# A hybrid four-mixer backbone on one core: own buffers for the gated branch, a fixed buffer layout, and other TensorE prices for the kernel's list scheduler

## The chip, the core and the metric

The kernel runs on one core of one Trainium2 chip. The metric is device time in microseconds (us) of one execution. Five engines work side by side, each in its own instruction order: TensorE (PE, matmuls; its weight loads appear as PEld), VectorE (DVE), ScalarE (ACT), GpSimd (POOL, here only an issuer of DMAs) and SyncE (SP, an issuer of DMAs).

## What is computed

Two layers work on 512 latent and 256 context tokens of width 1024. Each layer normalises and modulates its input to `h`, projects it, runs four token mixers side by side, and merges them through sigmoid gates:

```python
h = rmsnorm(x, norm_gain[l]) * (1.0 + scale) + shift
za, zb, zh, zf, zg = jnp.split(h @ w_in[l], SPLIT_IDX, axis=-1)
ya, yca = mixer_diff_attn(za, ...)     # differential attention, axial rotary
yb, ycb = mixer_neigh_attn(zb, ...)    # neighbourhood attention with a position bias
yh, ych = mixer_hgrn2(zh, ...)         # gated linear recurrence, both directions
yf = fourier_mix(zf)
x = x + gate * merge_branches(h, (ya, yb, yh, yf), zg, w_up[l], w_merge[l], w_out[l])

def merge_branches(h, ys, g, w_up_l, w_merge_l, w_out_l):
    for i in range(N_BRANCH):
        branch = (ys[i] * jax.nn.silu(gs[i])) @ w_up_l[i]
        term = jax.nn.sigmoid(h @ w_merge_l[i]) * branch
        acc = term if acc is None else acc + term
    return acc @ w_out_l
```

The context tokens go through the same weights; layer 1 needs them only as keys, values and state. Everything is float32.

## The kernel before

The large products are made three times over in the reduced float32 form (high x high, high x low, low x high): `split` (ACT for the high part, DVE for the low part) makes the two parts of each operand, and `mm3` issues the three products for each 128-row block. `h` is kept transposed in `h_hi` and `h_lo`. Weights arrive by SP into two buffers `wraw`, and are split into four buffers each of `wh` and `wl` ahead of their use. A product with `h` as the moving operand has 384 or 512 columns (`gemm_a`), one with a slice of `h` or of the merged result as the stationary operand has 256 (`gemm_b`, and the output projection).

The order of a layer as the program writes it: the projections of the recurrence, Fourier and differential branches; then four `merge` calls, one for each branch (Fourier, recurrence, differential, neighbourhood), with the projection of the neighbourhood branch (NA) ahead of the third; then the output projection, in whose last part the norm of the next layer begins. The four branches are generators (`ft_mix`, `hg_mix`, `da_mix`, `na_mix`); after each large product `unit_done` lets them take steps, and `need` completes a branch before its merge. NA starts once its keys are projected, so its steps lie beside the third merge, that of the differential branch.

`merge` (L1472) first makes the gated branch: gate product, tanh into `mth` (2 buffers), two DVE products, and a split into `ygs`, four tiles from the common buffers "u". Then for each of eight blocks it makes a merge-gate product, its tanh, an up projection of `ygs`, and adds to `acc`. In some blocks a set of eight 32-row matmuls makes modulation rows of the next layer or the output gate (`mod_rows`, by tiles `psg<-u,cst`).

None of this is the order that the chip runs. Each call is recorded as an `Op` (consecutive PE calls on one tile are one; `mm3` is cut into atoms of 4 x 3 matmuls), and `Program.order` is a list scheduler: again and again it takes the instruction that can start first, in the program's order among equals (weight transfers and splits count as 400 instructions earlier), by the prices in `Program.price` (L229) and by latencies. It looks at most 300 instructions past the oldest that is not done. An instruction that opens a new tile of a group ("tag") is taken only if a buffer is free and if the number of live tiles, counted in the program's order from the oldest open instruction on, stays within the buffers (`ok` in `order`). The most used group is "u", 31 buffers (`SLOTS`, L40) of 3072 bytes in each partition. The chosen order is emitted for each engine, which then runs strictly in it.

`emit` gives tiles their place in SBUF in the order of their first use, each padded to 32 bytes, behind 16384 bytes of descriptor space for POOL's DMAs. In the program so built, `wraw`, `wh` and `wl` start at multiples of 128 bytes, `h_hi` and `h_lo` 64 bytes past one, and the "u" buffers 96 bytes past one. PSUM is split into `psg` (3 buffers, large products), `psw` (2) and `pst` (1), for the branches.

Of the kernel before, what the change touches and what calls it, by code (L numbers as in the profile page):

```python
# [11 lines left out]
F32 = mybir.dt.float32  # L12
F32R = mybir.dt.float32r
# [8 lines left out]
P = 128  # L22
# [3 lines left out]
NT = NX + NC  # L26
# [10 lines left out]
MAIN_IN = (W_HF0, W_HQ, W_HI, W_FT, W_HF1, W_DAK, W_DAQ, W_DAV)  # L37
MERGE_ORDER = (3, 2, 0, 1)
NA_AT = 2
SLOTS = 31  # L40
RAW_BUFS = 2
W_BUFS = 4
PACE = 1.8
LEVELS = (64, 32, 16, 8, 4, 2, 1)
NA_KS = (0, 8, 24, 32)
NA_VAR = (0, 1, 1, 2)


class Tile:
# [120 lines left out]
class Program:  # L170
# [58 lines left out]
    def price(self, engine, method, args, kw):  # L229
        o = args[0]  # L230
        if method == "dma_start":
            return {"gpsimd": 1.0, "sync": 0.45, "scalar": 0.1}[engine]
        n = math.prod(o.shape[1:])
        if engine == "tensor":
            if method == "transpose":
                return 4 * args[1].shape[0] / 2400
            m = o.shape[0]
            slow = 4 if n >= m else 8 * m / n
            if args[2].dt != F32R and min(m, args[2].shape[0]) <= 64:
                slow = 2 * max(1, m / n)  # L240
            if args[2].dt == F32R:
                slow = 1 if n >= 2 * m else slow
            return (slow * n + 6) / 2400
        ins = [v for v in args[1:] if isinstance(v, View)]
        ps = any(v.tile.space == "ps" for v in ins + [o])
        n = max([n] + [math.prod(v.shape[1:]) for v in ins])
        if engine == "scalar":
            more = sum(isinstance(kw.get(k), View) for k in ("accum_out", "bias", "scale"))
            return (0.055 if ps else 0.095) + 0.09 * more + n / 1200
        two = len([v for v in ins if math.prod(v.shape[1:]) > 1]) > 1 or method == "tensor_reduce"  # L250
        if method == "reciprocal":
            return 0.07 + n / 160
        return 0.07 + n / (960 if two or ps else 1920)
# [82 lines left out]

    def emit(self, nc, pools):
        order = self.order()
        for op in order:
            for t in op.tiles:  # L340
                if t.real is None:
                    t.real = pools[t.space].tile(t.shape, t.dt, tag=t.tag, bufs=t.bufs, name=t.name)
            f = lambda v: v.real() if isinstance(v, View) else v
            for engine, method, args, kw in op.calls:
                getattr(getattr(nc, engine), method)(*map(f, args), **{k: f(v) for k, v in kw.items()})  # L345
        self.time = max(op.end for op in order)
# [3 lines left out]
def tile_hybrid_mixers(ctx, tc, io, out, dump=None):  # L350
    pools = {
        "sb": ctx.enter_context(tc.tile_pool(name="sb", bufs=1)),
        "ps": ctx.enter_context(tc.tile_pool(name="ps", bufs=1, space=PSUM)),
        "dram": ctx.enter_context(tc.tile_pool(name="dram", bufs=1, space=DRAM)),
    }
    ctx.enter_context(tc.manual_schedule())
    nc = Program()
# [9 lines left out]
    def nm(s):  # L367
        count[0] += 1
        return f"{s}_{count[0]}"

    def slot(shape=(P, NT), dt=F32):
        return mp.tile(list(shape), dt, tag="u", bufs=SLOTS, name=nm("u"))

# [36 lines left out]
    cols = cpool.tile([P, CO_N], F32, name="cols")  # L410
# [7 lines left out]
    masks = cpool.tile([P, len(LEVELS), P], I8, name="masks")  # L418
# [625 lines left out]
    def na_mix(l, z, res):  # L1044
# [2 lines left out]
        gn = sp.tile([P, 128], F32, tag="ngain", bufs=1, name=nm("ngain"))  # L1047
        nc.gpsimd.dma_start(gn, io["na_gain"][l:l + 1].partition_broadcast(P).rearrange("p a d -> p (a d)"))
        ts(gn[:, 0:64], gn[:, 0:64], 0.125)
        yT = [slot() for _ in range(2)]  # L1050
        res[1] = yT
        ntok = (6 if full else 4, 6)
        for i in (1, 0):
            yield from wait_for((l, "na", i))
            n = (3, ntok[i] - 3)
# [8 lines left out]
        for b in range(2):  # L1064
# [28 lines left out]
            k1, q1, q2 = (slot(dt=F32R) for _ in range(3))  # L1093
# [47 lines left out]
            def turn(cb, es):  # L1141
                w = 512 if cb < 4 else 256
                ps = psw()
                out = []
                for h in range(2):
                    for k in range(w // P):
                        transpose(ps[:, 512 * h + P * k:512 * h + P * (k + 1)], es[h][:, P * k:P * (k + 1)])
                for h in range(2):
                    eT = slot([P, 512])
                    act(eT[:, 0:w], ps[:, 512 * h:512 * h + w])  # L1150
                    out.append(eT)
                return out
# [319 lines left out]
    def merge(l, br, res, acc, first, last, fin, between):  # L1472
        rng = a_ranges(l == 0)
        wh, wl = chunk()
        yT = None
        ygs = [[slot(dt=F32R) for _ in range(2)] for _ in range(2)]
        for b in range(2):
            for n0, n1 in rng:
                ps = gemm_a(wh, wl, slice(P * b, P * (b + 1)), n0, n1)
                th = sp.tile([P, 512], F32, tag="mth", bufs=2, name=nm("mth"))[:, 0:n1 - n0]  # L1480
                act(th, ps, AF.Tanh, scale=0.5)
                stt(th, th, 1.0, ps, ALU.add, ALU.mult)
                stt(th, th, 0.5, res[br][b][:, n0:n1], ALU.mult, ALU.mult)
                split(ygs[b][0][:, n0:n1], ygs[b][1][:, n0:n1], th)
                unit_done(0.0103 * (n1 - n0))
        up = None
        for db in range(8):
            if db % 4 == 0:
                weights.release()
                if up is not None:  # L1490
                    weights.drop(1)
                up = [x.rearrange("p (b k c) -> p b k c", b=4, k=2) for x in weights.take()]
            wh, wl = chunk(1)
            if first:
                acc[db] = slot()
            if last:
                fin[db] = [slot(dt=F32R) for _ in range(2)]
            for n0, n1 in rng:
                ps = gemm_a(wh, wl, slice(0, P), n0, n1)
                th = sp.tile([P, 512], F32, tag="mth", bufs=2, name=nm("mth"))[:, 0:n1 - n0]  # L1500
                act(th, ps, AF.Tanh, scale=0.5)
                pu = psg()[:, 0:n1 - n0]
                mm3(pu, [(up[0][:, db % 4, k, :], up[1][:, db % 4, k, :], ygs[k][0][:, n0:n1], ygs[k][1][:, n0:n1]) for k in range(2)])
                a = acc[db][:, n0:n1]
                if first:
                    stt(a, th, 1.0, pu, ALU.add, ALU.mult)
                else:
                    stt(th, th, 1.0, pu, ALU.add, ALU.mult)
                    if last:
                        tt(th, th, a, ALU.add)  # L1510
                        split(fin[db][0][:, n0:n1], fin[db][1][:, n0:n1], th)
                    else:
                        tt(a, a, th, ALU.add)
                unit_done(0.0129 * (n1 - n0))
            between(db)
        weights.release()
        weights.drop(1)
# [6 lines left out]
    for l in range(DEPTH):  # L1524
# [44 lines left out]
        for j in range(4):  # L1569
            gt = gates[j]  # L1570
            cs = slice(256 * j, 256 * (j + 1))
            for u in range(2):
                n = min(3, nt - 3 * u)
                xn[j, u] = slot([P, 3, 256])
                nc.gpsimd.dma_start(xn[j, u][:, 0:n, :], xsrc[384 * u:384 * u + P * n, cs].rearrange("(t p) d -> p t d", p=P))
            wh, wl = chunk()
            for t in range(nt):
# [4 lines left out]
                u = sp.tile([P, 2, 256], F32, tag="q2", bufs=2, name=nm("gu"))[:, 0, :]  # L1582
# [127 lines left out]
```

## Time and profile before

| | |
|---|---|
| runs | 1517.60, 1518.24, 1518.64 us; median 1518.24 us |
| profiled execution | 1520.19 us, of which the span of its instructions 1518.4 us |
| PE busy | 1457.1 us, 96% of the span |
| DVE, ACT busy | 953.6 us (63%), 628.5 us (41%) |
| TensorE clock granted, mean | 0.988 of full |

The profile is one execution. Times in it count from the span's start. A tile `u<-mth` is an instruction that writes a tile of the group `u` and reads one of the group `mth`; since a helper records every operation, all instructions have the line L345, and tiles tell them apart. Matmul durations overlap, so how fast PE goes is read from the distance of starts or from the number in a stretch.

### The profile page before, as it was taken

The numbers are of one execution on the slowest core, as the hardware profiler recorded it, in microseconds if no ns is written. First come the engines' busy times: TensorE is split into PE (matmuls) and PEld (weight loads), VectorE is DVE, ScalarE is ACT, GpSimd is POOL, SyncE is SP. The second block draws the span as 40 slices with busy tenths as digits, with TensorE's granted clock in tenths as the row PEclk, the third lists the DMA queues.
The fourth block names the chain that finished last, engine by engine and source line by source line (L and its number), as shares of the span: only waits on it lengthen the run. The fifth ranks groups of instructions, "written<-read, shape, count | busy, mean of one in ns | idle before, by whom it ended". The sixth has DMA issues, their size and how long they took to land.

```text
span 1518.4 us, 25432 instructions
## 1 busy us (share of the span) xinstructions
PE 1457.1 (96%) x10068; PEld 1331.9 (88%) x10068; DVE 953.6 (63%) x2058; ACT 628.5 (41%) x1384; POOL 106.7 (7%) x207
## 2 busy tenths in 40 slices
PE   3999999999999997999999999999999999999998
PEld 2899989889999997889999999898887889888788
DVE  7794988577553355643444467979967855673544
ACT  5344454466522243431323244436445634552330
POOL 1000002210000010100001110000131000110000
PEclk9999999999999998999999999999999999999999
DMA  9211012332322142362222331211253222545332
GB/s 350 109 43 43 32 57 70 85 85 91 115 77 70 53 107 93 75 218 74 80 73 92 113 103 57 70 33 56 70 134 98 88 83 84 136 132 176 101 111 74
DMA packets 50599, 144.76 MB, mean 95 GB/s; under 512 B 7280, under 2 KB 12400, under 8 KB 50480
## 3 DMA queue, kind: packets, MB, share of 16 engines
q1 hardware_dynamic: 38336, 112.21, 22.7%
q0 software_dynamic: 12144, 30.93, 8.0%
q8 instruction: 79, 1.29, 0.3%
q14 instruction: 40, 0.33, 0.1%
HBM read 123.98 MB, written 4.19 MB: 84 GB/s over the span
## 4 chain that ended last, share of the span: by engine, by line
PE 85%; DVE 6%; ACT 5%; issue 2%; DMA 1%; SPq 0%; ACTq 0%; DVEq 0%; POOLq 0%
PE psg L345 69%; PE psw L345 11%; PE pst L345 4%; DVE u L345 3%; ACT u L345 3%; DVE sm L345 2%; ACT wh L345 1%; DMA u<-in_xin_dram 1%; ACT mth L345 0%; DVE wl L345 0%; DMA u<-in_rpb_dram 0%; DVE nss L345 0%; DVE psw L345 0%; SPq L345 0%; ACT h_hi L345 0%
## 5 line engine op out<-in xcount | busy, mean ns | idle before, releaser
L345 PE MATMUL psg<-h_hi,wh 128*128 128x384 f32 (+2 forms) x1216 | 439.6, 362 | 4.0 <-ACT mth L345 2.8
L345 PE MATMUL psg<-h_lo,wh 128*128 128x384 f32 (+2 forms) x1216 | 430.3, 354 | 0.2 <-DVE h_lo L345 0.2
L345 PE MATMUL psg<-h_hi,wl 128*128 128x384 f32 (+2 forms) x1216 | 430.4, 354 | 0.0
L345 DVE TENSOR_TENSOR wl<-wraw,wh 128x512 fp32r<-128x512 f32 x312 | 201.7, 686 | 175.8 <-ACT wh L345 174.9
L345 ACT ACTIVATE wh<-wraw 128x512 fp32r<-128x512 f32 x312 | 180.2, 624 | 244.7 <-PE psg L345 218.7
L345 PEld LDWEIGHTS psg<-h_hi,wh 128*128 128x128 f32 x1216 | 230.1, 189 | 24.9 <-ACT mth L345 5.7
L345 PEld LDWEIGHTS psg<-h_hi,wl 128*128 128x128 f32 x1216 | 229.8, 189 | 15.8
L345 PEld LDWEIGHTS psg<-h_lo,wh 128*128 128x128 f32 x1216 | 230.4, 189 | 14.8 <-DVE h_lo L345 0.5
L345 PE MATMUL psg<-wh,h_hi 128*128 128x256 f32 x544 | 156.3, 287 | 0.0
L345 PE MATMUL psw<-u,u 64*128 64x128 f32 (+6 forms) x1144 | 141.2, 299 | 12.3 <-ACT u L345 7.5
L345 PE MATMUL psg<-wl,h_hi 128*128 128x256 f32 x544 | 151.0, 278 | 0.0
L345 PE MATMUL psg<-wh,h_lo 128*128 128x256 f32 x544 | 150.9, 277 | 0.0
L345 ACT ACTIVATE u<-psw 128x768 f32<-128x768 f32 (+12 forms) x248 | 114.4, 485 | 81.3 <-PE psw L345 72.7
L345 PEld LDWEIGHTS psw<-u,u 64*128 64x128 f32 (+2 forms) x1144 | 113.1, 192 | 28.3 <-ACT u L345 13.2
L345 ACT ACTIVATE u<-psw,sm 128x768 f32<-128x768 f32 (+2 forms) x120 | 90.6, 758 | 88.9 <-DVE sm L345 75.7
L345 PE MATMUL psg<-wh,u 128*128 128x256 f32 x640 | 114.2, 280 | 0.9 <-ACT mth L345 0.9
L345 ACT ACTIVATE mth<-psg 128x384 f32<-128x384 f32 (+1 forms) x120 | 62.1, 519 | 127.8 <-PE psg L345 120.4
L345 DVE SCALAR_TENSOR_TENSOR mth<-mth,psg 128x384 f32<-128x384 f32 (+1 forms) x96 | 57.1, 595 | 91.0 <-ACT mth L345 73.9
L345 PE MATMUL psg<-u,wh 128*128 128x384 f32 (+1 forms) x384 | 107.6, 361 | 0.2 <-DVE u L345 0.2
L345 DVE TENSOR_REDUCE sm<-psw 128x1 f32<-128x768 f32 (+3 forms) x100 | 89.5, 901 | 26.1 <-PE psw L345 25.6
L345 PEld LDWEIGHTS psg<-wh,h_hi 128*128 128x128 f32 x544 | 102.2, 188 | 4.0
L345 POOL DMA_DIRECT2D u<-u x132 | 65.1, 505 | 568.8 <-ACT u L345 343.0
(128 smaller groups left out, 2002.9 us busy)
## 6 DMA issues: line engine op xcount, KB each, us to landing
wraw<-in_w_merge_dram SPq DMA_DIRECT2D x64, 512.0 KB, 3.6
wraw<-in_w_in_dram SPq DMA_DIRECT2D x60, 512.0 KB, 3.8
u<-in_w_mod_dram SPq DMA_DIRECT2D x32, 384.0 KB, 7.0
wraw<-in_w_up_dram SPq DMA_DIRECT2D x16, 512.0 KB, 3.5
wraw<-in_w_out_dram SPq DMA_DIRECT2D x16, 512.0 KB, 4.2
u<-u POOLq DMA_DIRECT2D x72, 96.0 KB, 2.4
u<-in_w_gate_dram SPq DMA_DIRECT2D x16, 384.0 KB, 6.3
u<-u POOLq DMA_DIRECT2D x24, 192.0 KB, 2.6
```

The source lines that it names most:

```text
L345: getattr(getattr(nc, engine), method)(*map(f, args), **{k: f(v) for k, v in kw.items()})
```

## The change

- The gated branch's four tiles get buffers of their own (group `yg`, 4 buffers of 3072 bytes).
- NA's output takes the buffer `dd` (6144 bytes), which the recurrence used alone before; NA's transposed attention weights take the two buffers `q2`, used so far by the rotary step and the output projection.
- "u" has 29 buffers instead of 31. The descriptor space of POOL's DMAs is 8192 bytes instead of 16384.
- Twelve groups get their place in SBUF first, in the order of the list `LAYOUT`.
- The scheduler's PE prices: a transpose has half its price; a reduced-form matmul costs its columns + 32 cycles of 2.4 GHz instead of columns + 6 (or four times the columns, where these were under twice the rows); one with at most 32 output rows costs its columns + 16 instead of twice the columns; others are as before up to a few cycles, and half where the output is one or two columns wide. The other engines' prices and the latencies stay.

```diff
-SLOTS = 31
+SLOTS = 29
+LAYOUT = ("cols", "masks", "ls2", "wraw", "wh", "wl", "ldl4", "nlam1", "hhi", "hlo", "u", "yg")
@@ price
             if method == "transpose":
-                return 4 * args[1].shape[0] / 2400
+                return 2 * args[1].shape[0] / 2400
             m = o.shape[0]
-            slow = 4 if n >= m else 8 * m / n
-            if args[2].dt != F32R and min(m, args[2].shape[0]) <= 64:
-                slow = 2 * max(1, m / n)
             if args[2].dt == F32R:
-                slow = 1 if n >= 2 * m else slow
-            return (slow * n + 6) / 2400
+                return (n + 32) / 2400
+            if m <= 32:
+                return (n + 16) / 2400
+            return (2 if min(m, args[2].shape[0]) <= 64 else 4) * max(n, m) / 2400
@@ emit
         order = self.order()
+        first = {}
+        for op in order:
+            for t in op.tiles:
+                first.setdefault(t.tag, t)
+        for tag in LAYOUT:
+            t = first[tag]
+            t.real = pools[t.space].tile(t.shape, t.dt, tag=t.tag, bufs=t.bufs, name=t.name)
@@ na_mix
-        yT = [slot() for _ in range(2)]
+        pair = mp.tile([P, 2, NT], F32, tag="dd", bufs=1, name=nm("yna"))
+        yT = [pair[:, b] for b in range(2)]
@@ na_mix, turn
-                    eT = slot([P, 512])
+                    eT = sp.tile([P, 512], F32, tag="q2", bufs=2, name=nm("eT"))
@@ merge
-        ygs = [[slot(dt=F32R) for _ in range(2)] for _ in range(2)]
+        ygs = [[mp.tile([P, NT], F32R, tag="yg", bufs=4, name=nm("yg")) for _ in range(2)] for _ in range(2)]
@@ kernel
-    nc = bacc.Bacc("TRN2", target_bir_lowering=False, num_devices=1)
+    nc = bacc.Bacc("TRN2", target_bir_lowering=False, num_devices=1, dynamic_dma_scratch_size=8192)
```

## Rows read from the trace of the kernel before

**Rows 1.** The page, busy us of each engine, share of the span, instructions.
```profile
PE 1457.1 (96%) x10068; PEld 1331.9 (88%) x10068; DVE 953.6 (63%) x2058; ACT 628.5 (41%) x1384; POOL 106.7 (7%) x207
```

**Rows 2.** Waits of PE, whole span: us in total, times, longest.
```profile
PE psg L345 <- DVE sm L345: 19.4, 1, 19.4
PE psw L345 <- ACT u L345: 18.1, 23, 2.9
...
PE psg L345 <- ACT mth L345: 6.6, 14, 0.5
```

**Rows 3.** Table of stretches: busy us (instructions), granted clock, DMA share, GB/s.
```profile
core 0: us, PE busy (x) PEld busy (x) DVE busy (x) ACT busy (x) POOL busy (x), PEclk, DMA share, GB/s
580.00:590.00 10.00, 10.00 (x66) 9.84 (x64) 5.03 (x10) 3.57 (x8) 0.00 (x0) 1.00 0.41 133
...
280.00:310.00 30.00, 25.94 (x157) 22.71 (x156) 19.57 (x42) 16.51 (x37) 5.58 (x12) 0.83 0.27 66
...
590.00:620.00 30.00, 21.18 (x140) 18.59 (x140) 16.55 (x35) 13.68 (x36) 2.31 (x5) 0.72 0.12 28
0.00:50.00 50.00, 25.34 (x210) 17.02 (x211) 36.71 (x95) 26.03 (x40) 5.66 (x14) 0.94 0.91 327
```

**Rows 4.** Timeline of DVE and ACT: start, length, instruction, idle before and its releaser.
```profile
406.53 0.56 DVE L345 SCALAR_TENSOR_TENSOR mth<-mth,u 128x384 f32<-128x384 f32 x1
...
407.12 0.53 ACT L345 ACTIVATE u<-mth 128x384 fp32r<-128x384 f32 x1 [0.80 <-DVE mth L345]
...
576.77 0.54 DVE L345 SCALAR_TENSOR_TENSOR mth<-mth,u 128x384 f32<-128x384 f32 x1
...
592.43 0.69 ACT L345 ACTIVATE u<-psw,sm 128x512 f32<-128x512 f32 x1 [4.29 <-DVE sm L345]
...
606.20 0.94 ACT L345 ACTIVATE u<-mth 128x384 fp32r<-128x384 f32 x2
```

**Rows 5.** Timeline of PE from 588 to 604 us.
```profile
588.94 1.11 PE L345 MATMUL psw<-u,u 128*128 128x256 f32 x8
...
593.93 1.97 PE L345 MATMUL psw<-kc,u 128*128 128x128 f32 x8 [2.86 <-ACT u L345]
597.08 2.08 PE L345 MATMUL psw<-u,u 128*128 128x256 f32 x8 [1.18 <-ACT u L345]
...
603.37 1.76 PE L345 MATMUL psw<-kc,u 128*128 128x128 f32 x8 [2.66 <-ACT u L345]
```

**Rows 6.** Chain that ended last, two pieces of large products: start, us, matmuls.
```profile
579.90 6.25 PE psg L345 x36
...
610.38 3.94 PE psg L345 x12
```

**Rows 7.** Timelines of PE and ACT: transposes; modulation rows, and ACT beside them.
```profile
557.79 1.47 PE L345 MATMUL psw<-kc,u 128*128 128x128 f32 x12
...
464.68 1.07 PE L345 MATMUL psg<-u,cst 128*32 128x256 f32 x16
466.24 0.61 PE L345 MATMUL psg<-kc,mrow 128*128 128x2 f32 x4 [0.49 <-ACT mth L345]
...
464.66 1.15 ACT L345 ACTIVATE wh<-wraw 128x512 fp32r<-128x512 f32 x2 [0.98 <-ACT wh L345]
```

**Rows 8.** Table of stretches: NA's projection, and the output projection of layer 0.
```profile
520.00:540.00 20.00, 20.00 (x179) 20.00 (x178) 10.24 (x22) 7.20 (x14) 0.00 (x0) 1.00 0.16 53
840.00:860.00 20.00, 20.00 (x173) 20.00 (x173) 9.88 (x31) 5.88 (x20) 3.25 (x6) 1.00 0.28 83
```

**Rows 9.** PE's groups by shape, output projections: busy us, mean ns of one.
```profile
L345 PE MATMUL psg<-wh,u 128*128 128x256 f32 x640 | 114.2, 280 | 0.9 <-ACT mth L345 0.9
L345 PE MATMUL psg<-wl,u 128*128 128x256 f32 x320 | 89.4, 279 | 0.0
```

**Rows 10.** The page: one kind of DMA issue with median us to landing; POOL's queue, packets, MB.
```profile
u<-in_w_mod_dram SPq DMA_DIRECT2D x32, 384.0 KB, 7.0
...
q0 software_dynamic: 12144, 30.93, 8.0%
```

## The prediction

> **What bounds the kernel now.** I read the page's busy shares first: TensorE (PE) is busy in 96% of the span, VectorE in 63% [rows 1]. So time goes away only where PE waits or where its work becomes faster; 1518.4 - 1457.1 = 61.3 us of the span is PE idle. Next, PE's list of waits [rows 2]: 19.4 us is one wait in the opening, before the first data is there; the rest lies in many waits on ScalarE (ACT) evictions, in stages where a branch's steps run between the large matmuls. Then the table of stretches [rows 3], which shows where they gather. From 580 to 590 us PE is full at the upper clock level. From 590 to 620 us it is busy 21.18 of 30 us, so 8.82 us idle, and the granted clock is 0.72: a mix of the two levels, 2.4 and 1.2 GHz. The only comparable stretch behind the opening is 280 to 310 us (4.06 us idle, 0.83).
>
> Last, the timelines of VectorE and ACT say why 590 to 620 us is so poor [rows 4]. In `merge`, after the gate's second product (`mth<-mth,u`) comes the split into the gated branch's high and low part (`u<-mth`). At 406 us the split starts 0.03 us after that product. The one made at 576.77 us ends at 577.31 and is split at 606.20, 28.9 us later, while ACT has idle time in between (4.29 us before one exponential); an earlier gate's split is in the same pair of splits at 606.20. Product and ACT were free, so what was missing is the target: those tiles come from the 31 buffers "u", and in that stage the neighbourhood attention (NA) of layer 0 holds them; counted by program order, all 31 are live there and at most 28 outside NA. The planner may not issue an instruction whose new tile would exceed the count. The gate temporaries (2 buffers `mth`) and PSUM tiles (3 `psg`) then fill up, no gate matmul can run, and PE is left with NA's own chain of scores, maximum, exponential, transpose, values: its transposes come at 593.93 and 603.37, one round in 9.4 us, with 2.86 and 2.66 us idle before them [rows 5].
>
> **Part by part.**
> *Own buffers for the gated branch (`yg`), NA's output in `dd`, its transposed weights in `q2`.* The split can then follow its product, the gates and up projections of that merge fill the chain's gaps, and the clock has no idle stretch to fall in. Worth at most: the 8.82 us idle, plus what ran slowly: the 8 score matmuls 2.08 instead of 1.11 us (+0.97), 8 transposes 1.97 and 1.76 instead of 8/12 of 1.47, that is 0.98 (+0.99 and +0.78) [rows 5, 7], 12 gate matmuls 3.94 instead of a third of 6.25, that is 2.08 (+1.86) [rows 6]. Sum 4.6, so 13.4 us. I take 12, as a covered chain still leaves short waits; the other end is 0. What moves forward is work that PE has to do anyway, and behind this stage PE is full with merges, so nothing else is late next. The transposed weights' two buffers add a wait: the eviction of a round needs the values of the round before to be done. PE runs values before the next transposes already (values sit between 588.94 and 593.93 [rows 5]); if it did bind, it costs the eviction's queue on ACT at most one group of score matmuls' length, 1.1 us, in the two or three rounds that are bound by the chain: 0 to 3 us, taken as 0. NA's output in `dd` waits for the recurrence of the same layer, which is complete before the second merge, and NA begins in the third: nothing.
>
> *Addresses (`LAYOUT`, smaller descriptor scratch).* Buffers are laid down in the order of first use, padded to 32 bytes. Before, the weights start at a multiple of 128 bytes, `h` 64 past one, "u" 96 past one. The new order gives 8192 + 128 of constants + 352 + 896 + 32 = 9600 = 75 x 128 for the weights, and 50624 and 99776 for `h` and "u", both 64 past a multiple of 128. The rows have a price for this, as far as it is the cause: with `h` stationary, 20 us hold 179 matmuls of 256 columns, with "u" stationary 173 [rows 8]; less the 2.4 that overlap the edges (0.28 us each [rows 9]) that is 113.3 and 117.2 ns. 960 such matmuls [rows 9] x 3.9 = 3.7 us. I take 3.5; the other end is 0, if the cause is another. The Trainium skill, "SBUF — State Buffer", Specifications, gives lines of 16 bytes, for which 32 and 64 past are alike; by that this term would be 0 and the sum 3.5 us smaller. The rows differ by 3.9 ns, so I keep the term.
>
> *Prices.* The planner took a transpose of 128 rows at 213 ns; 12 take 1.47 us with the pipeline's tail, about 108 each [rows 7], and the new price is 107. Eight 32-row matmuls of the modulation were 1.73 us, the trace has 1.07 with the tail [rows 7], new 0.91. The large ones go up by 26 columns, 10.8 ns (384 columns: 162.5 to 173.3; 36 took 6.25 us, 174 each [rows 6]). By program counts, 624 transposes x -0.107 = -67 us, 24 modulation sets x -0.82 = -20, about 7200 large matmuls x 0.0108 = +78: the plan's total hardly moves, its order does, everywhere. On the gaining side stand the 14 waits of 6.6 us for the tanh [rows 2]: PE ends the modulation earlier than planned and waits 0.49 us, as ACT had put a weight split of 1.15 us ahead of that tanh [rows 7]. On the losing side: large matmuls priced 6% low gave each chain 6% more cover than planned, and that cushion goes; a new hole as at 280 to 310 us costs 4.06 us idle [rows 3] and, in the proportion of the other hole (4.6 to 8.82), 2.1 us of slow work, 6.2 us in all. Between -6.6 and +6.2 no row is nearer to what a new order does: I take 0.
>
> *29 buffers "u" for 31.* In NA the moved tiles (4 gated, 2 outputs, 2 or more weights) free 8, so there are 6 more than before; outside NA and the merges there are two fewer. The tightest of these is the opening, where PE is busy 25.34 of 50 us and the DMA engines 0.91 of it [rows 3]: an input that waits for a buffer comes at most one landing later, 7.0 us [rows 10], and the queue behind it on SP (weights) with it. As the DMA engines are full there, the transfer would have waited anyway: 0, bounds 0 and +7. *Half the scratch:* 12144 packets in the whole run go through POOL's queue [rows 10], 759 to each of 16 engines. POOL has room; 0, at worst a landing or two of 2 to 4 us ahead of a head's stack.
>
> The sum: -12 - 3.5 + 0 + 0 = -15.5 us. The profiled execution took 1520.19 us (span 1518.4, 1.8 outside it), 1.95 above the median; the terms are differences, so they are set on the median: 1518.24 - 15.5 = 1502.7, rounded to **1503**. Ends of the terms: 1518.24 - 13.4 - 3.7 - 6.6 = 1494.5 with nothing lost.
>
> **Rivals.**
> *The hole closes in part.* Behind the freed split the next limit binds: NA's chain of 9.4 us for a round, or the two `mth` and three PSUM tiles, as VectorE and ACT serve NA and gates in one planned order. For it: ACT's idle before the exponential there ends on NA's own maximum, 4.29 us [rows 4]. Half of 12 with the address term: 1518.24 - 6 - 3.5 = 1508.7. Against it: at 406 us a split follows at once although another branch's steps run beside it [rows 4].
> *It doesn't do what it says.* The split waited for something else than a buffer, or the planner holds it back for another; then only the address term is left, 1514.7, or nothing, 1518.
> *Slower: thinner cover.* With true prices each chain gets just the planned cover, while ACT and VectorE prices stay as they are; holes like that at 280 to 310 us open in other mixed stages (the gated recurrence and the differential attention of both layers). Each costs 6.2 us; from the third on the gain of 15.5 is gone (2.5 x 6.2), and with four it is 1518.24 - 15.5 + 24.8 = 1527.5. For it: every chain's order is drawn anew. Against it: the plan now knows PE's progress, and the waits behind transposes and modulation were its errors.
> By the skill's line rule above the forecast would be 1506, inside the forecast's own range.
>
> **How the numbers follow.** Forecast (hole closed, own range 1494 to 1510): 0.55. Part: 0.17. No effect: 0.10. Slower: 0.18. A measurement of this kernel can tell about 0.2%, 3 us, from no change: 1515.2 to 1521.3 is "same". Faster gets 0.55 + 0.17 and 0.02 of the no-effect case (1514.7), 0.74; same 0.08; slower 0.18. The range 1492 to 1523 leaves out about 0.06 below and half of the slower case above.
>
> **What would show it.** Right: a tile `yg` written by ACT within about 1 us of each gate product; around 575 to 640 us PE full and the clock at 1.00; some 179 matmuls in 20 us of output projection instead of 173. Wrong: the chain of NA again with idle PE between its rounds, although the splits come at once (part); splits late again (no effect); clock digits under 9 in stages where there were none (slower).

## The result, and the profile after

| | before | after |
|---|---|---|
| median us (runs) | 1517.92 (1517.25 to 1518.64, 4) | 1493.33 (1492.88 to 1494.94, 4) |
| ratio, 95% interval | | 0.9841 (0.9826 to 0.9856) |
| profiled execution, span | 1520.19, 1518.4 | 1493.43, 1491.7 |
| PE busy, PE idle in the span | 1457.1, 61.3 | 1436.5, 55.2 |
| mean granted clock | 0.988 | 1.000 |

The time fell by 24.6 us; 15.5 us were predicted (1503). By the spans it is 26.7 us: 6.1 of them PE idle, 20.6 PE busy, that is the same 10068 matmuls done in less time. The page's line of engines, against [rows 1]:

```profile
PE 1436.5 (96%) x10068; PEld 1317.4 (88%) x10068; DVE 950.8 (64%) x2058; ACT 627.6 (42%) x1384; POOL 107.2 (7%) x207
```

PE's waits over the whole span (us in total, times, longest), against [rows 2]:

```profile
PE psg L353 <- DMA u<-in_w_mod_dram: 19.6, 1, 19.6
PE psw L353 <- DVE u L353: 10.5, 8, 6.8
PE psg L353 <- ACT mth L353: 6.6, 14, 0.5
PE psw L353 <- ACT u L353: 5.4, 9, 1.1
```

The waits for ACT's evictions fell from 18.1 us (23 times) to 5.4 (9 times). The 14 waits for the tanh are unchanged at 6.6 us. New is a wait of 6.8 us for DVE's `u`; it lies in the opening.

The table of stretches (busy us and instructions of PE, PEld, DVE, ACT, POOL; granted clock; DMA share; GB/s), against [rows 3] and, for the last line, [rows 8]:

```profile
0.00:50.00 50.00, 19.54 (x150) 13.68 (x150) 29.77 (x78) 20.80 (x32) 5.66 (x14) 1.00 0.92 326
280.00:310.00 30.00, 28.84 (x204) 26.99 (x203) 21.21 (x44) 18.18 (x40) 10.91 (x23) 1.00 0.45 100
590.00:620.00 30.00, 29.41 (x206) 27.99 (x204) 17.40 (x36) 12.79 (x30) 4.63 (x9) 1.00 0.61 166
820.00:840.00 20.00, 20.00 (x179) 20.00 (x178) 10.35 (x32) 6.07 (x21) 3.27 (x7) 1.00 0.32 95
```

Both poor stretches of before are gone: 590 to 620 us is busy 29.41 of 30 us at the upper clock level instead of 21.18 at 0.72, and 280 to 310 us has 28.84 instead of 25.94. The output projection holds 179 matmuls in 20 us instead of 173. The opening is worse: 19.54 us busy in the first 50, where before has 25.34; only four of the opening's eight modulation sets lie ahead of the first large matmul, in before all eight.

Timeline of DVE and ACT at a gate of the third merge, against [rows 4]:

```profile
574.17 0.55 DVE L353 SCALAR_TENSOR_TENSOR mth<-mth,u 128x384 f32<-128x384 f32 x1
...
574.76 0.53 ACT L353 ACTIVATE yg<-mth 128x384 fp32r<-128x384 f32 x1 [0.33 <-DVE mth L353]
```

The split follows its product by 0.04 us (28.9 us before). The chain that ended last shows what PE does there (start, us, tile, matmuls), against [rows 5, 6]:

```profile
575.64 2.08 PE psg L353 x12
577.72 1.02 PE pst L353 x16
578.74 2.13 PE psw L353 x16
580.88 2.08 PE psg L353 x12
582.96 1.02 PE pst L353 x16
```

One atom of 12 gate matmuls lies between NA's steps, and a round takes 5.2 us (577.72 to 582.96) instead of 9.4.

**Where the 26.7 us of the span lie.** Each kernel runs the same 6912 large matmuls that have weights as an operand (the 7200 of the prediction hold 288 reduced-form products of the branches too). The start of the n-th of them in two traces tells how far one kernel is ahead at that point of the work. Before starts its matmul number 0 at 48.0 us, 960 at 243.9, 1920 at 475.1, 2560 at 577.4, 2880 at 685.6, 4480 at 961.1, 6911 at 1514.3. Difference to that (us, negative is ahead), worked out from the starts in the traces, for after and for the kernels of the experiments:

| n | after | gated_31 | buffers_alone | prices_alone | transpose_price | large_price | transpose_large | layout_alone | after_squares |
|---|---|---|---|---|---|---|---|---|---|
| 0 (end of the opening) | -0.5 | +0.7 | +9.5 | -6.9 | -6.1 | +0.3 | -5.7 | +0.6 | -6.4 |
| 960 | +6.9 | +0.6 | +11.5 | -0.4 | -0.2 | +2.2 | +1.5 | +2.9 | +0.6 |
| 1920 (behind layer 0's differential attention) | -4.7 | -3.4 | +6.4 | -11.3 | +0.4 | +6.5 | -2.0 | -1.6 | -11.1 |
| 2560 (ahead of the hole) | -1.2 | -2.1 | +7.5 | -7.9 | +1.7 | +9.9 | +0.1 | -1.7 | -7.7 |
| 2880 (behind the hole) | -19.8 | -17.2 | -7.9 | -26.4 | +0.1 | -6.5 | -18.0 | -1.8 | -26.3 |
| 4480 (in layer 1) | -21.5 | -17.4 | -8.1 | -26.0 | -1.3 | -4.9 | -16.4 | -5.2 | -26.7 |
| 6911 (the last) | -26.7 | -15.2 | -6.9 | -22.7 | +3.2 | +2.6 | -16.7 | -8.1 | -32.6 |

The column layout_alone says how far to trust a step: that kernel has the same order of instructions as before, and still moves by +2.3 us from n = 0 to 960 and by -4.5 from 960 to 1920. The second step has a place. From 280 to 310 us before has PE busy 25.94 us at a clock of 0.83 [rows 3]; layout_alone is busy as long, at the upper level:

```profile
280.00:310.00 30.00, 25.92 (x181) 1.00 0.36 85
```

So the low clock there does not follow from the order and its idle time, and by estimate about 4 us of what the other columns gain from 960 to 1920 come from it, in the one execution of before that was profiled (gated_31, whose PE order is that of before up to 334 us, gains 4.0 there). Only larger steps, or steps with a wait behind them, are read. In after the hole gives 18.6 us (n = 2560 to 2880), the stage of the differential attention of layer 0 gives 11.6 (960 to 1920), so some 7 beyond that clock, and 7.4 are lost up to 960. The first is the place of the forecast; the others were not in its sum.

### The profile page after: what moved, and what is told of

The parts are those of the page before. It is cut to its first block, busy times and chain, and to the rows that moved or that the text cites. A ratio compares the mean times of both kernels' runs of the same rounds, so it can differ in the third digit from the quotient of the medians.

```text
span 1491.7 us, 25385 instructions
## 1 busy us (share of the span) xinstructions
PE 1436.5 (96%) x10068; PEld 1317.4 (88%) x10068; DVE 950.8 (64%) x2058; ACT 627.6 (42%) x1384; POOL 107.2 (7%) x207
## 4 chain that ended last, share of the span: by engine, by line
PE 86%; DVE 5%; ACT 4%; issue 2%; DMA 2%; SPq 1%; POOL 0%; ACTq 0%; DVEq 0%; POOLq 0%
PE psg L353 70%; PE psw L353 11%; PE pst L353 5%; DVE u L353 4%; ACT u L353 3%; ACT wh L353 1%; DMA u<-u 1%; SPq L353 1%; DVE sm L353 1%; DMA u<-in_w_mod_dram 1%; ACT mth L353 0%; DVE wl L353 0%; DVE nss L353 0%; DVE dd L353 0%; DVE h_lo L353 0%
## 5 line engine op out<-in xcount | busy, mean ns | idle before, releaser
L353 PE MATMUL psw<-u,u 64*128 64x128 f32 (+6 forms) x1144 | 135.4, 295 | 8.8 <-ACT u L353 3.1
L353 ACT ACTIVATE u<-psw 128x768 f32<-128x768 f32 (+10 forms) x208 | 93.8, 472 | 44.2 <-PE psw L353 40.9
L353 PE MATMUL psg<-wh,u 128*128 128x256 f32 x640 | 110.6, 277 | 0.9 <-ACT mth L353 0.9
L353 PE MATMUL psg<-yg,wh 128*128 128x384 f32 (+1 forms) x384 | 107.1, 360 | 0.0
L353 PEld LDWEIGHTS psg<-wl,h_hi 128*128 128x128 f32 x544 | 103.0, 189 | 0.2
L353 PEld LDWEIGHTS psg<-wh,h_lo 128*128 128x128 f32 x544 | 102.3, 188 | 0.0
```

## The experiments

Ratios are to the kernel before on the same chip, with the 95% interval. "Hole" is the stretch from 580 to 640 us, in which before has PE busy 50.05 of 60 us at a mean clock of 0.86.

| kernel | us | ratio | first large matmul at | PE busy in the hole, clock |
|---|---|---|---|---|
| buffers_alone | 1513.66 | 0.9971 (0.9957 to 0.9985) | 57.5 us | 59.45, 1.00 |
| prices_alone | 1498.08 | 0.9865 (0.9852 to 0.9878) | 41.1 | 59.35, 1.00 |
| layout_alone | 1512.1 | 0.9961 (0.9947 to 0.9974) | 48.7 | 49.76, 0.86 |
| buffers_prices | 1496.49 | 0.9854 (0.9841 to 0.9866) | 48.1 | 59.41, 1.00 |
| shared_33 | 1493.58 | 0.9832 (0.9818 to 0.9847) | 47.5 | 59.41, 1.00 |
| prices_layout | 1494.1 | 0.9837 (0.9823 to 0.9852) | 41.5 | 59.27, 1.00 |
| gated_31 | 1505.3 | 0.9907 (0.9890 to 0.9925) | 48.7 | 59.41, 1.00 |
| transpose_price | 1526.14 | 1.0048 (1.0031 to 1.0066) | 41.9 | 50.26, 0.86 |
| large_price | 1523.02 | 1.0036 (1.0021 to 1.0050) | 48.4 | 57.72, 1.00 |
| transpose_large | 1503.77 | 0.9890 (0.9873 to 0.9906) | 42.3 | 59.11, 1.00 |
| oldprices_squares | 1501.48 | 0.9892 (0.9878 to 0.9906) | 48.4 | 59.13, 1.00 |
| after_squares | 1488.88 | 0.9814 (0.9799 to 0.9829) | 41.6 | 59.41, 1.00 |

### The three parts, each alone

**buffers_alone**: the moved buffers, 29 "u" and the smaller scratch, with the old prices and no `LAYOUT`.

```diff
-SLOTS = 31
+SLOTS = 29
-        yT = [slot() for _ in range(2)]
+        pair = mp.tile([P, 2, NT], F32, tag="dd", bufs=1, name=nm("yna"))
+        yT = [pair[:, b] for b in range(2)]
-                    eT = slot([P, 512])
+                    eT = sp.tile([P, 512], F32, tag="q2", bufs=2, name=nm("eT"))
-        ygs = [[slot(dt=F32R) for _ in range(2)] for _ in range(2)]
+        ygs = [[mp.tile([P, NT], F32R, tag="yg", bufs=4, name=nm("yg")) for _ in range(2)] for _ in range(2)]
-    nc = bacc.Bacc("TRN2", target_bir_lowering=False, num_devices=1)
+    nc = bacc.Bacc("TRN2", target_bir_lowering=False, num_devices=1, dynamic_dma_scratch_size=8192)
```

> The kernel before with the moved buffers alone (gated branch, NA's output and transposed weights in buffers of their own, 29 common buffers, half the descriptor space); old prices, no fixed layout. If the buffers close the hole at 590 to 620 us and prices do the rest: near 1502 us (16 us less than before), no stretch of low clock around 600 us, and the stretch at 280 to 310 us still with some 4 us of idle PE. If the new prices closed the hole: near 1517 us, with the splits still late.

Measured: 1513.66 us. The hole is closed and the splits are prompt, but only 4.6 us are left at the end. The opening takes back 9.5 us. Timeline of ACT in the opening (the squares of the input, `u<-u`, start, length, idle before and its releaser), and two of PE's waits of the whole span:

```profile
12.83 0.84 ACT L345 ACTIVATE u<-u 128x768 f32<-128x768 f32 x1 [0.28 <-DMA u<-in_xin_dram]
21.57 3.78 ACT L345 ACTIVATE u<-u 128x768 f32<-128x768 f32 x5 [7.90 <-PE psg L345]
```

```profile
PE psg L345 <- DMA u<-in_w_mod_dram: 19.6, 1, 19.6
PE psw L345 <- DVE u L345: 10.9, 8, 6.8
```

After three squares ACT stands for 7.90 us, until PE has done with the first modulation weights at about 21.5 us. DVE's scaling and PE's transposes wait for the last five squares. So a part that was priced at 0 costs more than half of what the hole gives.

**prices_alone**: before with the new `price`, as in the diff of the change, and nothing else.

> The kernel before with the new TensorE prices alone. If the buffers close the hole: the hole in the third merge of layer 0 stays (a split 20 us or more behind its product), and the time is 1508 to 1518 us. If the prices do it: 1503 us or less without the hole. If true prices thin the cover (the slower rival): over 1521 us.

Measured: 1498.08 us, by far the largest part. The hole is closed although the buffers are as before. Timeline of DVE and ACT, then the chain that ended last:

```profile
567.54 0.55 DVE L344 SCALAR_TENSOR_TENSOR mth<-mth,u 128x384 f32<-128x384 f32 x1
...
582.79 0.94 ACT L344 ACTIVATE u<-mth 128x384 fp32r<-128x384 f32 x2
```

```profile
578.20 2.09 PE psg L344 x12
580.29 0.47 PE psw L344 x4
580.76 1.02 PE pst L344 x16
581.79 0.66 PE psw L344 x4
582.45 2.08 PE psg L344 x12
```

The split is still 14.7 us late (567.54 + 0.55 to 582.79). What changed is how the planner doles out the gate work that the late split allows: one atom of 12 between NA's steps. Before, 36 matmuls ran in one piece (6.25 us at 579.90 [rows 6]), 12 more at 587.01, and then none until 610.38. So a late split alone does not make a hole; a late split and lumps do.

**layout_alone**: before with `LAYOUT` (without `yg`) and the block in `emit`; every engine's order of instructions is that of before.

> The kernel before with the fixed order of buffers alone (without the group of the gated branch); the order of instructions stays as it was. If the start of the common buffers, 96 past a multiple of 128 bytes, costs 3.9 ns for each matmul of the output projection: some 3.5 us less, 1514 us, and 179 instead of 173 matmuls in 20 us of it. If lines of 16 bytes count: 1518 us.

Measured: 1512.1 us, 6.2 us less (4 to 8 by the interval). The table of stretches for PE, the same 20 us as in [rows 8]:

```profile
840.00:860.00 20.00, 20.00 (x179) 1.00 0.31 94
```

179 matmuls instead of 173: with the ends taken off as in the prediction, 113.3 instead of 117.2 ns. The 960 of them give 3.7 us. These matmuls do not explain the other 2.5; the clock from 280 to 310 us, above, is one place where executions of this order differ.

### Parts on top of each other

**buffers_prices**: after without `LAYOUT` and its block in `emit`.

> The changed kernel without the fixed layout. If addresses are worth what the row said: 1497 us, 3.5 us over the changed kernel. If not: 1493 us.

Measured: 1496.49 us; with `LAYOUT` it is after, 1493.33. The addresses are worth 3.2 us on top of the rest, though the two intervals overlap.

**prices_layout**: before with prices and `LAYOUT`, all buffers as before (31 "u").

> The kernel before with the new prices and the fixed layout, without any moved buffer, 31 common buffers. If the moved buffers add nothing once the prices are new: 1490 to 1494 us, no more than the changed kernel. If they are worth the hole in their own right: over 1500 us.

Measured: 1494.1 us, after gives 1493.33: with the prices new, the moved buffers bring nothing that can be measured. (Against prices_alone, which has the same order, the addresses give about 4 us: 1498.08 and 1494.1.) The moved buffers lose 6.4 us up to n = 960 (+6.9 against +0.5) and gain 5.2 behind the hole (from n = 2880 to the end -6.9 against -1.7). That gain is a second hole, which the new prices open in the differential attention of layer 1 as long as the buffers are those of before. PE in prices_layout, and then in after:

```profile
1110.00:1140.00 30.00, 27.30 (x159) 0.89 0.29 79
```

```profile
1110.00:1140.00 30.00, 30.00 (x200) 1.00 0.39 106
```

prices_alone has 27.30 at 0.89 there too; the 2.7 us idle are four waits for ACT's `u`. Before has no such hole (29.72 of 30 us, and 29.38 in the next 30, at 1.00). From n = 5120 to 5760 prices_layout goes from -27.9 to -24.3, prices_alone from -27.1 to -22.7, and after from -22.6 to -25.3.

**shared_33**: after with the gated branch back in the common buffers, of which there are 33.

```diff
-SLOTS = 29
+SLOTS = 33
-        ygs = [[mp.tile([P, NT], F32R, tag="yg", bufs=4, name=nm("yg")) for _ in range(2)] for _ in range(2)]
+        ygs = [[slot(dt=F32R) for _ in range(2)] for _ in range(2)]
```

> The changed kernel with the gated branch back in the common buffers, which are 33 for 29: the same bytes, shared. If the 29 buffers cost the opening some 7 us (the first large product at 47.5 us, with the prices and 31 buffers at 41.1), it starts near 41 us again and the time is 1486 to 1488 us, provided that the hole stays closed. If the opening's start is a chance of the order: within 3 us of 1493. If the gated branch needs buffers of its own: 1500 us or more, with the hole back.

Measured: 1493.58 us, the same as after. Whether the four tiles are separate makes no difference in the hole: among 33 common buffers, of which NA needs 29 by program order, the second gate's split is prompt as well (product from 573.76 to 574.31, split at 574.35). The opening is as late (47.5 us): the fifth square waits 6.77 us on PE. So a count of 29 is not the cause by itself; 33 with the other moves has the same wait, 31 without them has none.

**gated_31**: before with one part of the change, the gated branch's four own buffers; 31 "u" stay, and the scratch is 4096 bytes to make room.

> The kernel before with four own buffers for the gated branch and still 31 common ones (a quarter of the descriptor space), old prices and layout. If the late split makes the hole: closed, some 15 us; and if the 29 buffers were what delayed the opening by 9.5 us with the old prices, it starts at 48 us as before: 1502 to 1504 us. If the opening is delayed by the new order and not by the number of buffers: 1512 us.

Measured: 1505.3 us, 14.3 less (before was 1519.59 beside it). The opening stays at 48.7 us. The chain that ended last, in the place of the hole:

```profile
577.75 6.25 PE psg L345 x36
583.99 0.87 PE psw L345 x8
584.87 2.09 PE psg L345 x12
...
597.18 6.45 PE psg L345 x36
```

The lumps of 36 are still there, and PE is full all the same (stretch 590 to 620 us: 30.00 of 30), as the prompt splits let further gates and up projections follow. This is the mechanism of the forecast by itself, and its size: 15.1 us between n = 2560 and 2880. It also shows that the late opening comes with the other moves.

### Which price

**transpose_price**: before with the transposes' price alone.

```diff
-                return 4 * args[1].shape[0] / 2400
+                return 2 * args[1].shape[0] / 2400
```

> The kernel before with the new price of the transpose alone. If transposes at twice their length made the planner lump the gate products ahead of NA's rounds: hole closed, 1498 to 1505 us. If the large products' price did it: hole open, 1512 us or more.

**large_price**: before with the large products' price alone.

```diff
             if args[2].dt == F32R:
-                slow = 1 if n >= 2 * m else slow
+                return (n + 32) / 2400
```

> The kernel before with one price changed, that of the large products ((n + 32) instead of (n + 6) columns); transposes and modulation stay at their old prices, buffers and addresses as before. The old prices let the planner put 36 gate products at once between two steps of the neighbourhood attention; with all three new prices it puts 12 there, and the stretch from 580 to 640 us is full although the split is still late. Theory A (the large price alone thins these lumps, since a product counts 6% more cover): TensorE busy about 59 of 60 us there, and 1500 to 1505 us. Theory B (only the transposes' and the large price together do it, as a round of attention has to be priced shorter and the cover longer): the hole stays, about 50 of 60 us, and 1515 to 1520 us.

**transpose_large**: both of these; the modulation and the narrow products as before.

```diff
             if method == "transpose":
-                return 4 * args[1].shape[0] / 2400
+                return 2 * args[1].shape[0] / 2400
@@
+            if args[2].dt == F32R:
+                return (n + 32) / 2400
```

> The kernel before with two of the new prices: transposes and large products. The modulation's 192 products of 32 rows keep the old price (216 instead of 113 ns), as do 78 narrow products (at most 64 columns). Alone, the transposes' price gave 1526.1 (hole open, opening 6 us earlier) and the large products' price 1523.0 (hole closed, layer 1 lost 9 us); all new prices together 1498.1. Theory A (the two belong together: a chain's steps are mostly transposes on TensorE's side and its cover mostly large products, so that only with both right the cover has the length that the chain needs): 1498 to 1502 us, the stretch from 580 to 640 us full, layer 1 no longer slower than before. Theory B (each new order is a draw, in which one hole more or less comes out): anything between 1498 and 1526, with no stretch that is better for a reason; or the modulation's price is needed: 1515 us or more.

Measured: 1526.14, 1523.02 and 1503.77 us. Each alone is slower than before; together they gain 16.7 us (0.9890), and the full set, prices_alone, gains 20.2. The hole in the tables of stretches for PE, first transpose_price, then large_price, then transpose_large:

```profile
580.00:640.00 60.00, 50.26 (x339) 0.86 0.26 70
```

```profile
580.00:640.00 60.00, 57.72 (x448) 1.00 0.34 97
```

```profile
580.00:640.00 60.00, 59.11 (x448) 1.00 0.38 105
```

The hole belongs to the large products' price: alone it closes it (16.4 us between n = 2560 and 2880), the transposes' price does not (1.6). The start of the first large matmul belongs to the transposes' price (6.1 us earlier; large products' price 0.3 later), before and then transpose_price:

```profile
48.01 0.69 PE L345 MATMUL psw<-h_hi,wh 128*128 128x384 f32 x1
```

```profile
41.94 0.44 PE L345 MATMUL psw<-h_hi,wh 128*128 128x384 f32 x1
```

In before all eight of the opening's modulation sets (16 records each in PE's timeline) lie ahead of it, in transpose_price five, and the other three follow between the large products, at 43.19, 45.62 and 49.79 us. So most of this is work moved, not saved: at n = 160 transpose_price is only 1.7 us ahead, prices_alone 2.3, and at n = 960 0.2 and 0.4.

The loss of large_price lies ahead of the hole (9.9 us up to n = 2560) and in layer 1 (9.1 from 2880 to the end). That fits the rival of thinner cover, with the hole closed and the time still longer: products are priced near their true length, while transposes still count twice theirs. With both prices changed most of it is gone (+0.1 at n = 2560, 1.3 lost in layer 1). For large_price theory A had the hole right and the time wrong by 18 us, theory B nearly the reverse; for transpose_large theory A holds, 1.8 us beyond its range. Its theory B, that each new order is a draw, is not excluded for what lies outside the hole: these are four orders, and the large products' price with the modulation's was not tried.

Of what was tried, only the full set frees the stage of the differential attention of layer 0. PE's waits from 240 to 380 us in before, transpose_large and prices_alone:

```profile
PE psw L345 <- ACT u L345: 5.4, 10, 1.2
```

```profile
PE psw L345 <- ACT u L345: 4.7, 7, 1.2
```

```profile
PE psw L344 <- ACT u L344: 1.5, 3, 0.8
```

Transposes and large products leave the evictions' waits there nearly as they were; only with the modulation's (192 matmuls of 32 rows) and 78 narrow products' prices (38 are one or two columns wide, as in the list of the change, and 40 have 64 columns; all are halved) most of them go. Between n = 960 and 1920 prices_alone gains 10.9 us and transpose_large 3.5; as layout_alone gains 4.5 there without any new order, some 6 to 7 us are the prices' and none is left for transpose_large. Which of these two groups does it was not tried.

### The opening

**after_squares**: after, with the squares of the opening in the gated branch's buffers, which are idle there.

```diff
-                sq = slot([P, 3, 256])
+                sq = mp.tile([P, 3, 256], F32, tag="yg", bufs=4, name=nm("sq"))
```

> The changed kernel, with the opening's eight squares put into the four buffers of the gated branch, which are idle there, instead of the 29 common ones. Theory (a square waits for a common buffer that modulation weights hold until TensorE's first spread; in the changed kernel ACT stood 7.90 us for it, and TensorE's first transposes came at 37.6 instead of 29.8 us): the squares follow their inputs again, the first large product starts at about 41 us as in the kernels with 31 common buffers and the new prices, instead of 47.5, and the time is 1493.3 - 6 = about 1487 us. Rival (the opening is bound by the transfers anyway, or what comes early there waits in the recurrence): the first large product moves, but the end doesn't, or neither does: 1493.

Measured: 1488.88 us (1486.49 to 1491.89), the fastest of all. ACT's timeline in the opening, after and then after_squares:

```profile
12.86 0.84 ACT L353 ACTIVATE u<-u 128x768 f32<-128x768 f32 x1 [0.29 <-DMA u<-in_xin_dram]
21.60 3.78 ACT L353 ACTIVATE u<-u 128x768 f32<-128x768 f32 x5 [7.90 <-PE psg L353]
```

```profile
13.96 0.84 ACT L353 ACTIVATE sq<-u 128x768 f32<-128x768 f32 x1 [0.29 <-DMA u<-in_xin_dram]
...
18.52 0.84 ACT L353 ACTIVATE sq<-u 128x768 f32<-128x768 f32 x1 [0.27 <-DMA u<-in_xin_dram]
```

No square waits for PE any more (ACT is idle 0.27 to 0.34 us before each of the last six), PE's transposes behind the first three begin at 29.63 instead of 37.62 us, and the first large matmul at 41.6 instead of 47.5. The 5.9 us reach the end: the span is 5.7 us shorter, the median 4.5. So the squares' wait for a buffer was what the moved buffers cost.

**oldprices_squares**: the same with the old prices, that is buffers, addresses and squares without the prices.

> The changed kernel without its prices, with the opening's squares in the gated branch's buffers: moved buffers and addresses at the old prices. It tells what the prices are still worth where hole and opening are closed by other means. If the moved buffers alone lost 9.5 us in the opening through the squares' wait: 1513.7 - 9.5 - 4 (addresses) = about 1500 us, first large product at about 48 us; the prices are then worth some 13 us on top, of which 7 lie in the opening and the rest in the two differential attentions. If the opening of the kernel with moved buffers alone was late for another reason (weights in the queue behind inputs): 1509 us, first large product at about 57 us.

Measured: 1501.48 us, first large matmul at 48.4, as with 31 buffers at the old prices. With hole and opening mended by buffers, the prices are still worth 12.6 us (1501.48 - 1488.88). Of that the opening is only a small part: the 6.8 us at the first large matmul have shrunk to 1.8 at n = 960 (+2.4 against +0.6), as above. The differential attention of layer 0 gives 6.6 more (n = 960 to 1920: from +2.4 to -2.7 here, from +0.6 to -11.1 in after_squares), the hole 2.9 (15.7 here, 18.6 there), and what lies behind it 4.1 (from n = 2880 to the end -2.2 here, -6.3 there). My expectation put 7 us into the opening; that was wrong.

## Why the prediction was right and wrong

**The hole: place and mechanism right, its share in the sum only half the story.** The forecast took 12 us (13.4 at most) for own buffers; gated_31 measures 14.3, and 15.1 between the two points around the hole. It is above the upper end, as far as the rows show, because the sum stopped at 620 us and left out part of the slow work: NA's 16 value products take 1.63 and 1.98 us at 599.08 and 607.52, against 1.09 at 589.98, and are not in it. PE of before in short stretches:

```profile
605.00:610.00 5.00, 3.26 (x21) 0.50 0.00 0
610.00:615.00 5.00, 4.62 (x21) 0.61 0.00 0
...
620.00:630.00 10.00, 9.35 (x67) 1.00 0.66 162
630.00:640.00 10.00, 9.52 (x65) 1.00 0.01 2
```

Another 1.13 us is idle between 620 and 640 us (0.59 in gated_31), and from 605 to 615 us nearly all runs at the lower of the clock's two levels, 1.2 GHz, more than the matmuls that were counted. The rival that the hole closes in part, with NA's round of 9.4 us as the next limit, is wrong: the round was long because of the missing cover and the clock, and is 5.2 us in after.

What the forecast did not see is that the hole had two necessary conditions. It named the blocked split, and took "no gate matmul can run" as the whole cause. Of the gates that could run ahead of the block, the planner ran 36 matmuls in one lump, and that lump was a fault of the prices. Either remedy closes the hole (gated_31, prices_alone), so in after they overlap: the three parts alone give 4.6 + 20.2 + 6.2 = 31 us (before was 1518.28 beside these), together 24.6. That after's hole closed by own buffers, as the forecast has it, can't be said: shared_33 closes it without them, with room among 33 common buffers, and prices_layout with the split still 14.7 us late (product done at 569.42, split at 584.14).

**The addresses: right.** 3.5 us forecast; 6.2 measured alone, about 4 on top of the prices and 3.2 on top of the rest, with 179 matmuls in 20 us as foretold. The Trainium skill, "SBUF — State Buffer", Specifications, gives lines of 16 bytes, by which starts of 96 and 64 bytes past a multiple of 128 are alike and nothing would change; the trace does not agree, 117.2 against 113.3 ns. That it is the start of "u" alone was not tried: `LAYOUT` moves all groups at once.

**The prices: the failed step.** They were taken as 0 between -6.6 and +6.2. They are worth 20.2 us alone, about 17 on top of the moved buffers (1513.66 to 1496.49), 12.6 on top of buffers, addresses and squares. Three faults in the step:

- Its gaining end was one kind of wait, the 14 for the tanh, and these did not change at all (6.6 us in [rows 2] and in after).
- Its losing end priced a new hole like that at 280 to 310 us. The same row could be read the other way: that hole was there, in a mixed stage, and a better order can close it. It did; 25.94 us busy became 28.84. And the 2.1 us of slow work in that price rest on a clock of 0.83 that the same order does not have in layout_alone.
- It asked what a new order does to the stages without a hole, and not what the prices had to do with the hole itself. The lump of 36 stood in [rows 6], and the step on buffers had used it only for its duration.

The losing mechanism was real: large_price alone is 5.3 us slower (ratio 1.0036) with the hole closed, and transpose_price alone 6.6 (1.0048). With all prices changed together it came once, as the hole in the differential attention of layer 1 (prices_alone, prices_layout); it costs some 4 us, and with the moved buffers it is not there. The rival needed three or four such holes to cancel the gain. (280 to 310 us was not the only comparable stretch of before: behind the output projection, from 900 to 920 us, PE is idle 3.27 us. After has the like at 880 to 890 us, 3.35 us idle at 1.00, so none of the three parts reaches it.)

**29 buffers: sign and place right, the reason and the value wrong.** The bounds were 0 and +7, in the opening, and the value 0, as "the transfer would have waited anyway". It was no transfer that waited, but ACT's squares, for a buffer with modulation weights in it; 5.9 us with the new prices (47.5 to 41.6), 9.0 with the old (57.46 to 48.42). The count behind it was wrong too: by program order NA needs all 29 in after, not 8 fewer than the 31 of before, as the four gated tiles were not among the 31. The number 29 is not the cause by itself (shared_33).

**The sum.** Forecast -12 - 3.5 + 0 + 0 = -15.5. By the profiled executions: +6.9 up to n = 960 (6.3 of it the squares' wait: after_squares stands at +0.6 there), -11.6 in the differential attention of layer 0 (some 4.5 of it the clock of before's own execution, the rest the prices), +3.5 from there to the hole, -18.6 in the hole (buffers and prices, either of them enough for most of it), -6.9 behind it (about 3 of it the addresses, buffers_prices ends at -23.0). The range of 1492 to 1523 holds the time by 1.3 us; the forecast's own range, 1494 to 1510, does not. That it holds at all is partly luck: two terms were taken as 0 and went opposite ways, the prices' gain and some 6 us lost in the opening; with the squares in idle buffers the time is 1488.88, below the range.

**What stays open**: which of the modulation's and the narrow products' prices frees the differential attention of layer 0; which of the moved buffers keeps the hole in layer 1 away (the gated branch's own four are not needed: shared_33 has 29.82 of 30 us there, at 1.00); and why the opening's squares wait with 33 common buffers and the other moves, but not with 31 without them.

## What to carry to other kernels

A planner's prices are worth most where they decide how cover is dealt out: read from the trace how many matmuls lie in one lump beside a chain that starves, and correct all prices of an engine together, since one better price among false ones made this kernel slower, in both cases that were tried. When two changes aim at one hole, run each alone, because their gains do not add. When buffers move, follow in the opening who is first to ask for each, as compute may wait there for a buffer, not only transfers. Before a low clock in a stretch is put into a sum, look at a second execution of the same order.

## What was not expected of the hardware

- Start addresses count: with "u", the stationary operand, 96 bytes past a multiple of 128, a matmul of 256 columns takes 117.2 ns, 64 bytes past one 113.3 ns, in the same order of instructions (layout_alone). That "u" is the group that matters is likely, as the weights start at a multiple of 128 in both, but was not tried alone.
- The clock repaid more than the idle time. In the hole of before PE is idle 9.95 of 60 us at a mean clock of 0.86; closing it alone brings 15.1 us (gated_31, 59.41 busy at 1.00). By estimate the other 5 are work at the lower level beside the idle time, of which the prediction counted 4.6. Eight transposes that took 1.97 and 1.76 us there [rows 5] take 1.04 us in gated_31 in PE's timeline.
- The same order with the same idle time can have another clock: from 280 to 310 us before is busy 25.94 us at 0.83, layout_alone 25.92 at 1.00, gated_31 25.94 at 0.94, and layout_alone moves 4.5 us against before from n = 960 to 1920.
